# A trunk kernel on one core: the first shift and scale as TensorE products between projection steps, and a ring of 21 weight tiles

## The chip, the core and the metric

One Trainium2 chip, of which one core runs the whole program. The metric is the device time of one execution in microseconds (us). Three runs of the kernel before gave 1145.9, 1147.25 and 1149.82 us; the median is 1147.25.

## What is computed

One layer on 256 tokens of 1024 features, all float32. The conditioning vector c gives six rows (two shifts, two scales, two gates) of 1024 numbers each through one matrix of 1024 x 6144.

```python
mod = (jax.nn.silu(c) @ w_ada + b_ada).reshape(b, N_MOD, 1, d)
shift1, scale1, gate1, shift2, scale2, gate2 = (mod[:, i] for i in range(N_MOD))
h = rms_norm(x, norm1_g) * (1 + scale1) + shift1
proj = h @ w_in                                   # 1024 x 3078
# short convolution, stick-breaking attention and forgetting attention on parts of proj
x = x + gate1 * (y @ w_out)
h2 = rms_norm(x, norm2_g) * (1 + scale2) + shift2
return x + gate2 * moe_ffn(h2, ...)               # 32 experts, 4 for each token
```

## The kernel before

**Two stages.** The first (up to some 180 us) computes shift and scale, the normalized tokens, the projection, the three mixers, the output projection and the routing. The second goes through the 32 experts in order. The weights of one expert are twelve tiles of 1 MB (eight of the first matrix, four of the second), 128 partitions by 2048 numbers.

**The ring.** `big(kind, name)` gives a tile of 128 x 2048 out of one of four kinds, with the number of buffers in `KINDS` (line 33). The first stage uses the same buffers: kind "l" holds the tiles of `w_ada` (names a0 to a23) and `w_in` (w0 to w11), "h" the split projection weights and attention work tiles, "x" the normalized tokens and the like, "c" masks and the modulated tokens. The experts' tiles go round through the kinds in the order of the string `RING` (line 34), 20 long: tile n can be loaded when tile n - 20 has been used for the last time. `prefetch` issues the loads on SP's queue in program order, so a load that waits for a buffer holds up those behind it. An expert with more than 64 tokens has an extra block (`more`, for 32 tokens and further ones) that runs ahead of its ordinary pass and reads the same twelve tiles.

**The first projection.** Tokens are normalized (`xn`), turned on TensorE in four chunks of 256 features (`turn1(c)`, PSUM tile hTps), and modulated into `hT` with shift and scale of the chunk (`modulated1(c)`); `hT` is then split into two float32r parts, hTh by ScalarE and hTl by VectorE. `ada1(c)` gets the shift and the scale of one chunk on VectorE: `mod(m, c)` multiplies a half tile of `w_ada` with the row `silu_row` and adds up along it, four such passes in a chunk (line 236). A projection block (`Proj`, 256 columns of `w_in`) splits its weight tile into two parts (win0h, win0l, lines 109 and 110) and multiplies in 16 half steps of three products (`mm3`, 128 x 256 each, PSUM tile pr). `begin(c)` does the split, `steps(c, n)` the products up to chunk feature block n. `queue` fixes the order on TensorE: the products of a stage are issued after the last product of the stage ahead of it. The other engines' orders come from the scheduler of the framework. Loads are issued in the order of the string `order`.

Of the kernel before, what the change touches and what calls it, by code (L numbers as in the profile page):

```python
# [9 lines left out]
F32 = mybir.dt.float32  # L10
# [4 lines left out]
ALU = mybir.AluOpType  # L15
# [3 lines left out]
P = 128  # L19
# [10 lines left out]
CH = 2048  # L30


KINDS = {"l": 7, "h": 8, "x": 2, "c": 3}
RING = "lhhllccchlhhhxhhlllx"
CAP = 64
MORE = ((64, 32), (96, 64), (160, 64), (224, 32))

# [12 lines left out]
def trunk(ctx: ExitStack, tc: tile.TileContext, x_d, p1_d, p2_d, be_d, ada_d, win_d, wout_d, w1_d, w2_d, out_d):  # L50
# [8 lines left out]
    def big(kind, name):  # L59
        return ring.tile([P, CH], F32, tag=kind, bufs=KINDS[kind], name=name)  # L60

# [9 lines left out]
    def pa(name):  # L71
        return psA.tile([P, 2, 512], F32, tag="A", name=name)
# [9 lines left out]
    def mm(out, lhsT, rhs, start, stop):  # L82
        last[:] = [nc.tensor.matmul(out, lhsT, rhs, start=start, stop=stop, skip_group_check=True).ins]  # L83
# [101 lines left out]
    qkSB = big("x", "qkSB")  # L185
    v = big("x", "v").rearrange("p (t n) -> p t n", t=NT)
    ada, win, wout = {}, {}, {}
    order = "a0 a4 w0 a1 w6 a5 a2 a6 a3 a7 p0 w1 p1 w2 w3 w7 a8 a12 w4 a16 a9 w8 w5 a17 a10 a13 a11 w9 a14 a18 w10 a20 a15 w11 a19 a22 a23 a21 o1 o2 o3"
    for name in order.split():
        kind, c = name[0], int(name[1:])  # L190
        if kind == "p":
# [27 lines left out]
    nc.vector.tensor_mul(silu, silu, p1[:, C_C:C_C + KD])  # L219

    silu_row = t4o("silurow")
    ps = pa("silurow").rearrange("p b n -> p (b n)")
    for k in range(KD):
        mm(ps[:, k * P:(k + 1) * P], silu[:, k:k + 1].to_broadcast([P, P]), ident, True, True)
    nc.scalar.copy(silu_row[:, 0:512], ps[:, 0:512])
    nc.vector.tensor_copy(silu_row[:, 512:D], ps[:, 512:D])

    mods = const.tile([P, 6, KD], F32, name="mods")
    bada = p1[:, C_BC:C_BC + 48].rearrange("p (m k) -> p m k", m=6)
# [1 line left out]
    def mod(m, c):  # L231

        w = ada[4 * m + c].rearrange("p (i k) -> p i k", i=2)
        for i in range(2):
            k = 2 * c + i
            nc.vector.scalar_tensor_tensor(w[:, i], w[:, i], 1.0, silu_row, op0=ALU.mult, op1=ALU.mult,  # L236
                                           accum_out=mods[:, m, k:k + 1])
# [6 lines left out]
    def shift_scale(m, c, gain):  # L244

        biased(m, 2, c)
        cs = slice(2 * c, 2 * c + 2)
        nc.vector.scalar_tensor_tensor(mods[:, m + 1, cs], mods[:, m + 1, cs], 1.0, p1[:, gain + 2 * c:gain + 2 * c + 2],
                                       op0=ALU.add, op1=ALU.mult)
# [20 lines left out]
    def turn1(c):  # L270
        turned1[c] = pb(f"hTps{c}").rearrange("p (k s) -> p k s", k=2)
        for i in range(2):
            for t in range(NT):
                k = 2 * c + i
                turn(turned1[c][:, i, t * P:(t + 1) * P], xn[:, t, k * P:(k + 1) * P])

    def ada1(c):
        for m in range(2):
            mod(m, c)
        shift_scale(0, c, C_N1)  # L280

    def modulated1(c):

# [47 lines left out]
                                           gains[:, 2 * mixer + j:2 * mixer + j + 1],  # L331
                                           sq[:, j * S:(j + 1) * S], op0=ALU.mult, op1=ALU.mult)

    def two(t):
        return t[:, 0:768].rearrange("p (h s) -> p h s", h=2), t[:, 1024:1792].rearrange("p (h s) -> p h s", h=2)

    def sb_scores(pair):
        q, k = qk[0][:, 2 * pair, :], qk[0][:, 2 * pair + 1, :]
        ps = pa(f"sb{pair}")
        for blk in range(2):  # L340
            for j in range(2):
                r = slice(64 * j, 64 * j + 64)
                if blk == 0:
                    mm(ps[:, j, 0:256], k[r, 0:P], q[r, :], True, False)
                else:
                    mm(ps[:, j, 256:384], k[r, P:S], q[r, P:S], False, True)
        z = ps[:, :, 0:384]
        e, r = two(big("h", f"sbt{pair}"))
        nc.scalar.activation(e, z, AF.Abs)
        nc.scalar.activation(e, e, AF.Exp, scale=-1.0)  # L350
        nc.scalar.activation(e, e, AF.Ln, bias=1.0)
        nc.vector.scalar_tensor_tensor(r, z, 0.0, e, op0=ALU.max, op1=ALU.add)
        for b in (0, 2):
            blk_ = r[:, :, b * P:(b + 1) * P]
            nc.vector.tensor_mul(blk_, blk_, LT.rearrange("p (o s) -> p o s", o=1).to_broadcast([P, 2, P]))
        return ps, e, r
# [149 lines left out]
                   first and i == 0, last and i == len(ks) - 1)  # L506


    two_ps = pa("pr17")
    early = {}  # L510

    def begin(c, ps=None):
        early[c] = Proj(c, ps)

    def steps(c, n=KD):
        early[c].steps(n - early[c].k)

    queue(lambda: turn1(0),
          lambda: ada1(0),
          lambda: begin(0),  # L520
          lambda: turn1(1),
          lambda: modulated1(0),
          lambda: ada1(1),
          lambda: modulated1(1),
          lambda: begin(6),
          lambda: steps(0, 4),
          lambda: turn1(2),
          lambda: ada1(2),
          lambda: turn1(3),
          lambda: steps(6, 4),  # L530
          lambda: modulated1(2),
          lambda: ada1(3),
          lambda: steps(0, 6),
          lambda: modulated1(3),
          lambda: steps(6, 6),
          lambda: begin(1, two_ps[:, 0, :]),
          lambda: steps(1, 6),
          lambda: steps(0),
          lambda: steps(6),
# [562 lines left out]
def _layout(inp):  # L1102
# [34 lines left out]
    pick += [(256, 128), (512, 128), (384, 128), (640, 128), (0, 256)]  # L1137
    win = np.concatenate([w_in[:, a:a + n] for a, n in pick], axis=1)

    def blocks(w, n):  # L1140
        return w.reshape(KD, P, -1, n).transpose(2, 1, 0, 3).reshape(-1, P, KD * n)

    return {
        "x": f["x"][0], "p1": p1, "p2": np.stack([fw, rw]), "be": be,
        "ada": f["w_ada"][0].reshape(D, 24, 2, P).transpose(1, 3, 2, 0).reshape(24, P, CH), "win": blocks(win, 256),
        "wout": f["w_out"][0].reshape(4, 2, P, D).transpose(0, 2, 1, 3).reshape(4, P, CH),
        "w1": w1,
        "w2": f["w_mlp2"][0].reshape(NE, 4, 2, P, D).transpose(0, 1, 3, 2, 4).reshape(NE, 4, P, CH),
# [16 lines left out]
```

## Time and profile before

| | us |
|---|---|
| median of three runs | 1147.25 |
| the profiled execution | 1146.89 |
| span of its instructions | 1144.9 |
| PE busy (share of the span) | 1069.5 (93%) |
| DVE busy | 389.2 (34%) |
| ACT busy | 178.6 (16%) |
| mean transfer rate | 393 GB/s |

PE is TensorE's matmul side, DVE is VectorE, ACT is ScalarE, SP issues most loads. The profile is of one execution; a product's end is modelled, so two records that start 0.12 us apart can each be shown as 0.28 us long, and the spacing of starts is what a product costs. Float32 products are shown as two records each, float32r products as one. PEclk is the granted clock of TensorE: 1.00 is 2.4 GHz and 0.50 is 1.2 GHz.

### The profile page before, as it was taken

The numbers are of one execution on the slowest core, as the hardware profiler recorded it, in microseconds if no ns is written. First come the engines' busy times: TensorE is split into PE (matmuls) and PEld (weight loads), VectorE is DVE, ScalarE is ACT, GpSimd is POOL, SyncE is SP. The second block draws the span as 40 slices with busy tenths as digits, with TensorE's granted clock in tenths as the row PEclk, the third lists the DMA queues.
The fourth block names the chain that finished last, engine by engine and source line by source line (L and its number), as shares of the span: only waits on it lengthen the run. The fifth ranks groups of instructions, "written<-read, shape, count | busy, mean of one in ns | idle before, by whom it ended". The sixth has DMA issues, their size and how long they took to land. (4 is left out here: it accounts for less than half of the span.)

```text
span 1144.9 us, 14101 instructions
## 1 busy us (share of the span) xinstructions
PE 1069.5 (93%) x5432; PEld 467.1 (41%) x5432; DVE 389.2 (34%) x879; ACT 178.6 (16%) x412; POOL 14.5 (1%) x52
## 2 busy tenths in 40 slices
PE   2999999999989999999999989999999999898987
PEld 2887844343333333433333433434343434242322
DVE  7799933222232223222222222232232322231222
ACT  3458622010101010101010100101010101010100
POOL 1000000000000000000000000000000000000000
PEclk7899999999999999999999989999999999999999
DMA  9888899999987999999999999999999999999992
GB/s 383 360 297 311 331 409 370 416 418 417 418 353 309 417 418 417 418 418 417 417 418 416 419 399 404 419 418 418 417 417 419 417 418 417 411 416 410 416 413 110
DMA packets 62913, 449.54 MB, mean 393 GB/s; under 512 B 6960, under 2 KB 7472, under 8 KB 8624
## 3 DMA queue, kind: packets, MB, share of 16 engines
q1 hardware_dynamic: 62336, 447.11, 95.6%
q8 instruction: 79, 1.29, 0.5%
q10 hardware_dynamic: 432, 0.59, 0.1%
q14 instruction: 66, 0.54, 0.1%
HBM read 446.63 MB, written 1.05 MB: 391 GB/s over the span
## 5 line engine op out<-in xcount | busy, mean ns | idle before, releaser
L83 PE MATMUL u<-we,xg 128*64 128x512 f32 (+1 forms) x2304 | 494.2, 577 | 12.7 <-DMA we<-in_w 11.3
L83 PEld LDWEIGHTS u<-we,xg 128*64 128x64 f32 (+1 forms) x2304 | 154.0, 134 | 299.9 <-issue 260.4
L83 PE MATMUL o<-we,aT 128*64 128x512 f32 x1024 | 236.5, 598 | 3.7 <-DMA we<-in_w 3.3
L891 DVE TENSOR_SCALAR sw<-u 128x256 f32<-128x256 f32 (+1 forms) x68 | 28.3, 417 | 441.6 <-PE u L83 429.5
L892 ACT ACTIVATE sw<-sw 128x256 f32<-128x256 f32 (+1 forms) x68 | 27.9, 411 | 666.8 <-DVE sw L891 666.8
L83 PEld LDWEIGHTS o<-we,aT 128*64 128x64 f32 x1024 | 69.6, 136 | 133.2 <-issue 121.8
L1088 DVE TENSOR_TENSOR o<-o,g 64x512 f32<-64x512 f32 x64 | 44.1, 689 | 162.2 <-PE o L83 161.7
L83 PE MATMUL y<-o,sc 128*128 128x512 f32 (+1 forms) x160 | 67.1, 592 | 2.1 <-DVE o L1010 1.3
L83 PEld LDWEIGHTS xg<-oh,xn 128*128 128x128 f32 x512 | 58.6, 192 | 12.6 <-issue 12.4
L83 PE MATMUL xg<-oh,xn 128*128 128x128 f32 x512 | 62.1, 279 | 0.1
L236 DVE SCALAR_TENSOR_TENSOR a<-a,silurow 128x1024 f32<-128x1024 f32 x48 | 57.2, 1216 | 0.0
L745 DVE TENSOR_SCALAR xg<-xg,mods 128x128 f32<-128x128 f32 x64 | 26.0, 410 | 62.7 <-ACT xg L748 61.5
L83 PE MATMUL u<-b,pick 128*128 128x512 f32 x64 | 31.0, 484 | 17.3 <-PEq L1021 16.7
L83 PEld LDWEIGHTS y<-o,sc 128*128 128x128 f32 (+1 forms) x160 | 26.5, 197 | 41.8 <-issue 33.4
L944 DVE TENSOR_TENSOR xr<-xr,y 128x1024 f32<-128x1024 f32 x30 | 36.6, 1221 | 11.8 <-PE y L83 10.4
L904 ACT COPY aT<-aT 128x256 f32<-128x256 f32 x64 | 23.8, 372 | 106.1 <-PE aT L86 106.0
L748 ACT ACTIVATE xg<-xg,mods 128x128 f32<-128x128 f32 x64 | 28.9, 457 | 56.4 <-PE xg L83 45.9
L83 PEld LDWEIGHTS u<-b,pick 128*128 128x128 f32 x64 | 12.1, 189 | 57.1 <-issue 55.9
L86 PEld LDWEIGHTS aT<-ident,a 128*128 128x128 f32 x128 | 14.2, 141 | 50.7 <-issue 33.9
L895 DVE TENSOR_TENSOR a<-a,sw 128x256 f32<-128x256 f32 x64 | 27.4, 428 | 6.8 <-ACT sw L892 0.3
L86 PE MATMUL aT<-ident,a 128*128 128x128 f32 x128 | 27.2, 294 | 2.0
L83 PE MATMUL op<-o,yT 128*128 128x512 f32 x64 | 29.0, 600 | 0.0
(299 smaller groups left out, 750.3 us busy)
## 6 DMA issues: line engine op xcount, KB each, us to landing
we<-in_w SPq DMA_DIRECT2D x383, 1024.0 KB, 19.9
a<-in_ada SPq DMA_DIRECT2D x24, 1024.0 KB, 7.0
w<-in_win SPq DMA_DIRECT2D x12, 1024.0 KB, 11.0
o<-in_wout SPq DMA_DIRECT2D x4, 1024.0 KB, 5.8
xr<-in_x SPq DMA_DIRECT2D x1, 1024.0 KB, 5.3
we<-in_w SPq DMA_DIRECT2D x2, 512.0 KB, 18.1
b1in<-in_be SPq DMA_DIRECT2D x1, 512.0 KB, 5.3
out<-xr SPq DMA_DIRECT2D x2, 256.0 KB, 2.0
```

Source lines behind the costliest of these rows:

```text
L83: last[:] = [nc.tensor.matmul(out, lhsT, rhs, start=start, stop=stop, skip_group_check=True).ins]
L86: last[:] = [nc.tensor.transpose(out, in_, ident).ins]
L236: nc.vector.scalar_tensor_tensor(w[:, i], w[:, i], 1.0, silu_row, op0=ALU.mult, op1=ALU.mult, accum_out=mods[:, m, k:k + 1])
L745: nc.vector.tensor_scalar(o, x, s2[:, k:k + 1], t2[:, k:k + 1], op0=ALU.mult, op1=ALU.add)
L748: nc.scalar.activation(o, x, AF.Identity, scale=s2[:, k:k + 1], bias=t2[:, k:k + 1])
L891: nc.vector.tensor_scalar(gl, u[:, 0:n], 7.0, None, op0=ALU.min)
L892: nc.scalar.activation(sg, gl, AF.Sigmoid, scale=1.702)
L895: nc.vector.tensor_mul(ln, ln, sg)
L904: nc.scalar.copy(aT.rearrange("p j s -> p (j s)"), ps[:, 0:n])
L944: nc.vector.tensor_add(xr[:, t, :], xr[:, t, :], y.rearrange("p h m -> p (h m)"))
L1088: nc.vector.tensor_mul(o[64 * (e % 2):64 * (e % 2) + 64, 512 * h:512 * h + 512], ps[r, :], g2[r, :])
```

## The change

The first shift and scale leave VectorE. `ada1(c)` is now 32 products: for each of the eight blocks of the contraction and each of four groups q, the silu column repeated 32 times is the weight and a 128 x 128 piece of a `w_ada` tile (laid out anew on the host, so that a chunk's shift and scale lie in two tiles) is the data; the four groups write four bands of 32 partitions of one PSUM tile. A 32 x 32 block transpose on VectorE brings the sums to the features' partitions, and two small operations add the bias and the gain as before. `warm(n)` issues n products of the identity with itself into a PSUM bank that nobody reads. The products of `silu_row` move into the queue. The queue's stages and the order of the loads are new, and the ring has one "l" buffer more: 21 tiles in another order of kinds. `two` is renamed `halves`.

```diff
-KINDS = {"l": 7, "h": 8, "x": 2, "c": 3}
-RING = "lhhllccchlhhhxhhlllx"
+KINDS = {"l": 8, "h": 8, "x": 2, "c": 3}
+RING = "llhhllccchhhhxxhhllll"
...
-    order = "a0 a4 w0 a1 w6 a5 a2 a6 a3 a7 p0 w1 p1 w2 w3 w7 a8 a12 w4 a16 a9 w8 w5 a17 a10 a13 a11 w9 a14 a18 w10 a20 a15 w11 a19 a22 a23 a21 o1 o2 o3"
+    order = "a0 a1 w0 a2 a3 w6 a4 a5 w1 a6 a7 w7 p0 w2 p1 a8 a12 w3 a16 a9 w4 w8 w5 a17 a10 a13 a11 w9 a14 a18 w10 a20 a15 w11 a19 a22 a23 a21 o1 o2 o3"
...
+    two_ps = pa("pr17")
+    def warm(n):
+        for i in range(n):
+            mm(two_ps[:, 1, 0:P], ident, ident, True, True)
...
+    mods_ps = pa("mods")
     def ada1(c):
-        for m in range(2):
-            mod(m, c)
-        shift_scale(0, c, C_N1)
+        ps = mods_ps[:, c % 2, c // 2 * P:(c // 2 + 1) * P]
+        for k in range(KD):
+            w = ada[2 * c + k // 4].rearrange("p (k q n) -> p k q n", k=4, q=4)[:, k % 4]
+            for q in range(4):
+                mm(ps[32 * q:32 * q + 32, :], silu[:, k:k + 1].to_broadcast([P, 32]), w[:, q], k == 0, k == KD - 1)
+        t = sm.tile([P, P], F32, tag="sc", name=f"modsT{c}")
+        nc.vector.transpose(t, ps)
+        cs = slice(2 * c, 2 * c + 2)
+        nc.vector.tensor_tensor(mods[:, 0:2, cs], t.rearrange("p (m k i) -> p m k i", m=2, k=2)[:, :, :, 0],
+                                bada[:, 0:2, cs], op=ALU.add)
+        nc.vector.scalar_tensor_tensor(mods[:, 1, cs], mods[:, 1, cs], 1.0, p1[:, C_N1 + 2 * c:C_N1 + 2 * c + 2],
+                                       op0=ALU.add, op1=ALU.mult)
...
-    queue(lambda: turn1(0),
+    queue(lambda: warm(12),
+          silu_rows,
+          lambda: turn1(0),
+          lambda: turn1(1),
           lambda: ada1(0),
+          lambda: modulated1(0),
           lambda: begin(0),
-          lambda: turn1(1),
-          lambda: modulated1(0),
+          lambda: warm(8),
+          lambda: steps(0, 2),
+          lambda: warm(4),
           lambda: ada1(1),
           lambda: modulated1(1),
           lambda: begin(6),
+          lambda: warm(8),
+          lambda: turn1(2),
           lambda: steps(0, 4),
-          lambda: turn1(2),
+          lambda: steps(6, 2),
           lambda: ada1(2),
+          lambda: modulated1(2),
           lambda: turn1(3),
           lambda: steps(6, 4),
-          lambda: modulated1(2),
+          lambda: begin(1, two_ps[:, 0, :]),
+          lambda: steps(1, 4),
+          lambda: steps(0, 6),
           lambda: ada1(3),
-          lambda: steps(0, 6),
           lambda: modulated1(3),
           lambda: steps(6, 6),
-          lambda: begin(1, two_ps[:, 0, :]),
           lambda: steps(1, 6),
...
```

How the instructions move: TensorE at the start of the program, before (silurow is the silu row in PSUM, hTps a chunk of turned tokens, pr a projection block, xn the normalized tokens).

```order
L83 MATMUL silurow<-ident,silu 128x128 x8
L86 MATMUL hTps_265<-ident,xn 128x128 x4
L86 MATMUL hTps_283<-ident,xn 128x128 x4
L83 MATMUL pr_276<-hTh,win0h 128x256
L83 MATMUL pr_276<-hTl,win0h 128x256
```

The same place now (pr_234 is the PSUM tile that takes the fillers and the silu row, mods the sums of the new products, a_140 to a_148 tiles of `w_ada`).

```order
L83 MATMUL pr_234<-ident 128x128 x12
L83 MATMUL pr_234<-ident,silu 128x128 x8
L86 MATMUL hTps_277<-ident,xn 128x128 x4
L86 MATMUL hTps_282<-ident,xn 128x128 x4
L83 MATMUL mods<-a_140,silu 32x128 x16
L83 MATMUL mods<-a_142,silu 32x128 x16
L83 MATMUL pr_234<-ident 128x128 x8
L83 MATMUL pr_329<-hTh,win0h 128x256
```

Fillers and the first group of 32-column products now stand ahead of the first projection product; after twelve projection products four more fillers and the second group follow.

VectorE between the silu row and the second chunk, before (a_140 to a_152 are tiles of `w_ada`, w_144 and w_148 weight tiles that are split).

```order
L226 COPY silurow<-silurow 128x512
L236 SCALAR_TENSOR_TENSOR a_140,mods<-a_140,silurow 128x1024 x2
L236 SCALAR_TENSOR_TENSOR a_142,mods<-a_142,silurow 128x1024 x2
L110 TENSOR_TENSOR win0l<-w_144,win0h 128x1024
L242 TENSOR_TENSOR mods<-mods,p_74 128x2x2
L110 TENSOR_TENSOR win0l<-w_144,win0h 128x1024
L248 SCALAR_TENSOR_TENSOR mods<-mods,p_74 128x2
L236 SCALAR_TENSOR_TENSOR a_146,mods<-a_146,silurow 128x1024
L287 TENSOR_SCALAR hT<-hTps_265,mods 128x256 x2
```

And now.

```order
L237 COPY silurow<-pr_234 128x512
L110 TENSOR_TENSOR win0l<-w_144,win0h 128x1024 x2
L299 STREAM_TRANSPOSE modsT_319<-mods 128x128
L301 TENSOR_TENSOR mods<-modsT_319,p_74 128x2x2
L303 SCALAR_TENSOR_TENSOR mods<-mods,p_74 128x2
L311 TENSOR_SCALAR hT<-hTps_277,mods 128x256 x2
L313 TENSOR_TENSOR hTl<-hT,hTh 128x256 x2
L299 STREAM_TRANSPOSE modsT_392<-mods 128x128
L301 TENSOR_TENSOR mods<-modsT_392,p_74 128x2x2
L110 TENSOR_TENSOR win6l<-w_150,win6h 128x1024
L303 SCALAR_TENSOR_TENSOR mods<-mods,p_74 128x2
L110 TENSOR_TENSOR win6l<-w_150,win6h 128x1024
```

The passes over `w_ada` are gone from this stretch; the split of w0 now stands ahead of the first chunk's sums, and the split of w6 between the second chunk's sums and its hT.

## Rows read from the trace of the kernel before

**Rows 1.** The page's slices: the span in 40 equal parts of 28.6 us, GB/s moved.
```profile
GB/s 383 360 297 311 331 409 370 416 418 417 418 353 309 417 418 417 418 418 417 417 418 416 419 399 404 419 418 418 417 417 419 417 418 417 411 416 410 416 413 110
```
**Rows 2.** Stretches of the span: start and end, length, busy time (and instructions) of PE, PEld, DVE, ACT and POOL, granted clock, busy share of the sixteen transfer engines, GB/s.
```profile
35.00:58.70 23.70, 23.24 (x191) 21.40 (x190) 16.82 (x32) 10.70 (x18) 0.00 (x0) 1.00 0.81 326
58.70:171.00 112.30, 110.64 (x694) 83.50 (x693) 87.89 (x192) 66.07 (x143) 0.00 (x0) 1.00 0.90 342
180.00:340.00 160.00, 154.88 (x865) 61.54 (x865) 41.31 (x102) 17.57 (x44) 2.54 (x6) 1.00 1.00 409
342.00:349.00 7.00, 6.24 (x25) 2.10 (x26) 3.73 (x10) 0.00 (x0) 0.00 (x0) 0.76 0.01 4
356.00:640.00 284.00, 277.03 (x1269) 104.88 (x1269) 73.44 (x163) 26.68 (x67) 2.66 (x10) 1.00 1.01 418
1121.00:1134.00 13.00, 11.05 (x49) 3.25 (x47) 1.60 (x4) 0.79 (x2) 0.00 (x0) 1.00 0.07 30
```
**Rows 3.** Waits of SP's load queue between 310 and 352 us: for whom, us in total, times, longest.
```profile
SPq L858 <- PE u L83: 34.5, 6, 24.2
```
**Rows 4.** Timeline of PE between 303 and 352 us: start, length, engine, line, what it writes from what, count (xg gathers the tokens of the extra block; u with 64 columns is the ordinary pass).
```profile
323.00 1.07 PE L83 MATMUL xg<-xn,ox 128*32 128x256 f32 x16
...
344.68 0.47 PE L83 MATMUL u<-b,pick 128*128 128x512 f32 x1 [0.67 <-PEq L1021]
345.08 7.46 PE L83 MATMUL u<-we,xg 128*64 128x512 f32 x26
```
**Rows 5.** The chain that ended last, its end in order of time: start, length, what.
```profile
1112.57 19.88 DMA we<-in_w
1132.44 0.14 issue
...
1140.94 0.69 DVE xr L1098
```
**Rows 6.** The page's costliest groups: line, engine, operation, what from what, shape, count, busy us, mean ns of one, idle time before them.
```profile
L83 PE MATMUL xg<-oh,xn 128*128 128x128 f32 x512 | 62.1, 279 | 0.1
L236 DVE SCALAR_TENSOR_TENSOR a<-a,silurow 128x1024 f32<-128x1024 f32 x48 | 57.2, 1216 | 0.0
```
**Rows 7.** Timeline of PE in the first 36 us.
```profile
6.19 3.75 PE L83 MATMUL silurow<-ident,silu 128*128 128x128 f32 x16 [6.19 <-DVE silu L219]
...
10.37 1.04 PE L86 MATMUL hTps<-ident,xn 128*128 128x128 f32 x7 [0.21 <-DVE xn L265]
20.51 0.58 PE L83 MATMUL pr<-hTh,win0h 128*128 128x256 f32 x1 [9.10 <-ACT hTh L288]
22.00 0.58 PE L83 MATMUL pr<-hTl,win0h 128*128 128x256 f32 x1 [0.91 <-DVE hTl L289]
...
30.22 0.58 PE L83 MATMUL pr<-hTh,win0h 128*128 128x256 f32 x1 [5.51 <-ACT hTh L288]
```
**Rows 8.** Timeline of PE between 163 and 180 us (lg is the router's product, xg tokens gathered for the first two experts).
```profile
166.91 0.65 PE L83 MATMUL lg<-h2T,rw 128*32 128x128 f32 x16
...
174.36 1.06 PE L83 MATMUL xg<-oh,xn 128*128 128x128 f32 x8
```
**Rows 9.** The router's products by tile: ns of one (lowest, median, highest), first and last start.
```profile
L83 PE MATMUL lg<-h2T,rw x32: 272/273/298, 166.9 to 175.7; 128*32 128x128 f32 x32
```
**Rows 10.** Timeline of ACT between 13 and 31 us.
```profile
13.61 1.99 ACT L109 CAST win0h<-w 128x1024 fp32r<-128x1024 f32 x2 [3.04 <-DMA w<-in_win]
18.59 1.04 ACT L109 CAST win6h<-w 128x1024 fp32r<-128x1024 f32 x1 [2.99 <-DMA w<-in_win]
20.05 0.86 ACT L288 CAST hTh<-hT 128x256 fp32r<-128x256 f32 x2 [0.42 <-DVE hT L287]
```
**Rows 11.** Timeline of DVE between 13.5 and 31 us.
```profile
15.92 1.22 DVE L110 TENSOR_TENSOR win0l<-w,win0h 128x1024 fp32r<-128x1024 f32 x1
...
19.48 0.99 DVE L287 TENSOR_SCALAR hT<-hTps,mods 128x256 f32<-128x256 f32 x2
```
**Rows 12.** Groups of DVE between 300 and 350 us by shape: count, busy us, mean ns, idle before.
```profile
L953 DVE STREAM_TRANSPOSE xg<-xg 128x256 f32<-128x256 f32 x1 | 0.5, 451 | 0.0
```
**Rows 13.** Timeline of PE between 58 and 66 us (qkss is the sum of squares of two heads); pr<-hTh,win2h at 58.67 is the first product after the fourth projection block.
```profile
58.67 0.28 PE L83 MATMUL pr<-hTh,win2h 128*128 128x256 f32 x1
...
59.27 0.28 PE L83 MATMUL pr<-hTh,win2l 128*128 128x256 f32 x1
59.58 1.13 PE L83 MATMUL qkss<-qksq,masks 128*128 128x512 f32 x2
...
60.66 0.28 PE L83 MATMUL pr<-hTl,win2h 128*128 128x256 f32 x1
```
**Rows 14.** Stretches of 1 us, columns as in rows 2 (the granted clock is the third number from the end).
```profile
13.00:14.00 1.00, 0.00 (x0) 0.00 (x0) 1.00 (x3) 0.40 (x1) 0.00 (x0) 0.97 0.97 401
14.00:15.00 1.00, 0.00 (x0) 0.00 (x0) 1.00 (x3) 1.00 (x2) 0.00 (x0) 0.50 0.98 410
...
34.00:35.00 1.00, 1.00 (x9) 1.00 (x8) 1.00 (x4) 0.00 (x0) 0.00 (x0) 0.79 1.00 415
```
**Rows 15.** Waits of PE between 58 and 180 us: for whom, us in total, times, longest.
```profile
PE pr L83 <- DVE win5l L110: 0.8, 1, 0.8
...
PE pr L83 <- ACT win5h L109: 0.4, 1, 0.4
PE pr L83 <- DVE win3l L110: 0.3, 1, 0.3
```

More of the change, by code (lines that the diff above doesn't have):

```diff
@@ L221, in trunk, with silu_rows @@
     silu_row = t4o("silurow")
[L222 to L226, printed above, removed]
+    two_ps = pa("pr17")
+    def warm(n):
+        for i in range(n):
+            mm(two_ps[:, 1, 0:P], ident, ident, True, True)
+    def silu_rows():
+        ps = two_ps.rearrange("p b n -> p (b n)")
+        for k in range(KD):
+            mm(ps[:, k * P:(k + 1) * P], silu[:, k:k + 1].to_broadcast([P, P]), ident, True, True)
+        nc.scalar.copy(silu_row[:, 0:512], ps[:, 0:512])
+        nc.vector.tensor_copy(silu_row[:, 512:D], ps[:, 512:D])
     mods = const.tile([P, 6, KD], F32, name="mods")
@@ L275, in turn1 @@
                 turn(turned1[c][:, i, t * P:(t + 1) * P], xn[:, t, k * P:(k + 1) * P])
+    mods_ps = pa("mods")
     def ada1(c):
-        for m in range(2):
-            mod(m, c)
-        shift_scale(0, c, C_N1)
+        ps = mods_ps[:, c % 2, c // 2 * P:(c // 2 + 1) * P]
+        for k in range(KD):
+            w = ada[2 * c + k // 4].rearrange("p (k q n) -> p k q n", k=4, q=4)[:, k % 4]
[8 more added lines that the diff above has]
+                                       op0=ALU.add, op1=ALU.mult)
     def modulated1(c):
@@ L332, in qk_norm, with halves @@
                                            sq[:, j * S:(j + 1) * S], op0=ALU.mult, op1=ALU.mult)
-    def two(t):
+    def halves(t):
         return t[:, 0:768].rearrange("p (h s) -> p h s", h=2), t[:, 1024:1792].rearrange("p (h s) -> p h s", h=2)
@@ L347, in sb_scores @@
         z = ps[:, :, 0:384]
-        e, r = two(big("h", f"sbt{pair}"))
+        e, r = halves(big("h", f"sbt{pair}"))
         nc.scalar.activation(e, z, AF.Abs)
@@ L506, in out_proj @@
                    first and i == 0, last and i == len(ks) - 1)
-    two_ps = pa("pr17")
     early = {}
@@ L1138, in _layout @@
     win = np.concatenate([w_in[:, a:a + n] for a, n in pick], axis=1)
+    shift_scale = f["w_ada"][0][:, 0:2 * D].reshape(2, 4, P, 2, 4, 2, 4, 32)
+    shift_scale = shift_scale.transpose(4, 0, 2, 1, 6, 3, 5, 7).reshape(8, P, CH)
     def blocks(w, n):
@@ L1144, in _layout @@
         "x": f["x"][0], "p1": p1, "p2": np.stack([fw, rw]), "be": be,
-        "ada": f["w_ada"][0].reshape(D, 24, 2, P).transpose(1, 3, 2, 0).reshape(24, P, CH), "win": blocks(win, 256),
+        "ada": np.concatenate([shift_scale, f["w_ada"][0][:, 2 * D:].reshape(D, 16, 2, P).transpose(1, 3, 2, 0).reshape(16, P, CH)]),
+        "win": blocks(win, 256),
         "wout": f["w_out"][0].reshape(4, 2, P, D).transpose(0, 2, 1, 3).reshape(4, P, CH),
```

## Prediction

> **What bounds the kernel now.** I read the slices first. Loads run at 416 to 418 GB/s in most slices, but at 297 to 360 in four of the first five and at 353 and 309 in the two that meet at 343 us [rows 1]. So transfers are the limit for most of the span, and what has to be found is where they stop and what restarts them.
>
> The table of stretches answers that [rows 2]. From 180 to 340 us PE is busy 154.88 of 160 us, and its waits there name almost only its own branches, none a weight: PE sets the pace and the ring of weight tiles is full. From 342 to 349 us 4 GB/s are moved: the transfers stand still. SP sat 24.2 us on one product of the first expert layer [rows 3]: the extra block of 32 tokens (323.00 to 344.68 us) reads its expert's twelve tiles and the ordinary pass reads them again, so nothing is released until 345.08 plus four products at half clock [rows 4]. From 356 to 640 us the rate is 418 GB/s. At the end 30 GB/s, 0.07 of sixteen engines, run on from 1121 to 1134 us: one of the sixteen engines is about 13 us behind, though all had stopped together at 342 us. So from about 349 us to the last landing at 1132.44 us the slowest engine has work all the time, and some 10 us of products and additions follow [rows 5]. Two things move the end: **when PE releases the first tile after the stop**, and **how many tiles were loaded before it**. A stop that only some engines feel (near 680 us) moves nothing.
>
> Going back from there, PE has hardly a pause down to 35 us: busy 110.64 of 112.3 us and 23.24 of 23.7 [rows 2]. The chain therefore begins in the first 35 us, where VectorE is busy without a break: each shift or scale pass over half a tile takes 1216 ns, 16 such passes stand there [rows 6], and PE gets its first projection product at 20.51 us and the second chunk's at 30.22 us [rows 7].
>
> **The change, part by part.** The profiled execution took 1146.89 us (span 1144.9), 0.36 us under the median of 1147.25; the sum is made against 1146.89.
>
> *A. Shift and scale on PE.* Sixteen passes leave VectorE (16 x 1.216 = 19.5 us). Four groups of 32 products come, 32 columns of weights and 128 of data. The router's products have exactly this shape: 16 records (8 products) in 0.65 us, each lasting 0.273, so (0.65 - 0.273)/15 = 0.025 us a record, 0.05 us a product at full clock, and a group 1.6 us [rows 8, 9]. A filler is a 128 x 128 product: 0.22 us at full clock (8 records in 1.06 us, each 0.279), 0.47 at half clock (8 in 3.75) [rows 6 to 8].
>
> The first chunk: w0 is still the fourth MB in the queue, so its casts still start at 13.61; w0 and w6 are two loads and 4.98 us apart, 2.5 us a load [rows 10]. The first subtraction can start at 14.65, the second ends at 17.0 (1.2 us each [rows 11]); VectorE's transpose of 128x256 takes 451 ns [rows 12], so I take 0.25 for 128x128, plus 0.15 for two small operations, 0.5 for hT and 0.43 for its cast: the first projection product starts at 18.3 instead of 20.51. The fillers and the first group are over by about 14.8 (turned tiles 11.4, group 1.6, eight fillers 1.8), so PE then stands 3.5 us.
>
> The second chunk waits for 12 products, 4 fillers and its group. At full clock that is 18.3 + 0.45 (wait for hTl) + 1.45 + 0.9 + 1.6 = 22.7; with the first two at half clock 24.8; with all at half clock 26.4. VectorE then needs transpose and small operations 0.5, both halves of w6 (they stand ahead of hT in its order) 2.3, hT 0.5, and the cast 0.43: 3.7 us. PE starts on the second chunk at 26.4, 28.5 or 30.1.
>
> From there PE is dense. 180 products x 0.12 = 21.6 (spacing of [rows 13]); two more groups 3.2; a turn 0.5; waits for hTl 0.7; the forget gate's eight products, of twice the router's columns, 0.8, its turn with the wait for ScalarE's copy 1.3 (an estimate from the copies' 0.4 us); two qkss 1.9 (less than twice 1.15); changes of product kind some 0.6: 30.6 us. The end is 57.0, 59.1 or 60.7. Before, the same work ends at 58.67 plus 1.15 for the second qkss (59.27 to 60.66 less two spacings) [rows 13]: 59.8. So A gives +2.8, +0.7 or -0.9 us. It is small because PE, relieved of waiting, takes on 6.4 us of groups itself, and most of the 30 us are needed either way. I take **+0.7**: the granted clock fell to 0.50 at 13.9 us, 2.6 us after PE's last product, and came back only at 34.4 us, after PE had worked from 30.2 us [rows 14]; a gap of 3.5 us is nearest to that. Ends: -1.5 and +2.8.
>
> The Trainium skill, "TensorE: Matmul & The Clock Gate", Part 3, gives 3.07x for four tiles packed by rows and 2.38x for three packed by columns, not the full number. By that a group would cost 32 x 0.22/3.07 = 2.3 us, an estimate from that page, and A would be lower by about 2 us; the rows of this trace show 0.22/0.05 = 4.4x for this very shape, so the sum goes by them.
>
> *B. What follows.* Between 58 and 171 us PE waits 0.8, 0.4 and 0.3 us for splits of w5 and w3 [rows 15]. VectorE has its split of w7 done near 46 us (after hT of the last chunk near 43) instead of 53.4, does w2 and four gate passes (2.4 + 4.9) while PE is in the fourth block, and waits some 3 us for the forget gate; it so reaches w3 about 2 us earlier. I count **+1.0** of the 1.5; ends 0 and 1.5. The order inside that stage changes little, and its loads get earlier.
>
> *C. One more tile.* At 342 us the queue stands for 7 us, and one more load takes 2.5 us, so it fits into the stop; every later release then serves a tile one place further on. From there the slowest engine is never idle, so the end comes **2.5 us** earlier; ends 0 and 2.5. What hides the tile before 300 us is that PE waits for no weight there: the earlier loads themselves win nothing. For the same reason the new order of kinds costs nothing: SP now comes to both x buffers as 14th and 15th tile and waits there until the output projection is through with its weights (near 167 us), with the l tiles behind it, where it waited at the 16th before; without that cover each load held back would cost 2.5 us.
>
> Moved loads: a2 and a3 stand ahead of w6, w1 and w7 ahead of the gates. Each is wanted later than its place times 2.5 us says (a7 lands at 33.6, PE wants it near 40). Layout work on the host and the renamed helper cost nothing on the device.
>
> Sum: 0.7 + 1.0 + 2.5 = 4.2, so 1142.7, and on the scale of the median **1143.0 us**; own range 1141 to 1145.
>
> **The rivals.**
> 1. *The fillers do not hold the clock.* PE's pause after 14.8 us lets it fall, and 12 products, 4 fillers and the whole group run at 1.2 GHz: A is -0.9 and B shrinks to 0.6; 2.2 us remain, 1145.0. For it: [rows 14]; the products that began at 22.0 us did not raise it before [rows 7]. Against: work would start earlier and be longer. The same page of the Trainium skill, Part 1, has half rate as the default that activity releases and idleness brings back. By that rule, with which the rows agree, the first filler groups are spent for nothing. Chance 0.20.
> 2. *The tile counts nothing.* If transfers, not releases, bind from 180 us on, or the slowest engine is idle again later, C is 0 and 1.7 us remain: 1145.5. Against: 4 GB/s over 7 us. Chance 0.10.
> 3. *All goes well.* The clock stays full, the waits for splits vanish: 2.8 + 1.5 + 2.5 = 6.8, 1140.5. Chance 0.14.
> 4. *Slower: the 32-column products do not overlap.* At 0.22 us a product a group costs 7.0 instead of 1.6 us on PE, with the projection steps queued behind it; the first has some 4 us of room, so 1.4 + 3 x 5.4 = 17.6 us later: 1160.6. It turns the sign past the 3.4 us of "no change" from about 0.13 us a product. Against: the router's 0.05. Chance 0.08.
>
> **How the numbers follow.** The forecast has 0.48. A measurement here can tell about 0.3% (3.4 us) from no change, so "faster" is below 1143.8: about two thirds of the forecast (0.33), rival 3 (0.14) and a little of the first two (0.02): 0.49. Same: the rest of the forecast and of rivals 1 and 2: 0.43. Slower: rival 4, 0.08. The range reaches from the third rival less 1.7 us (runs spread by some 2 us to either side) to the case in which A is -1.5 and C is 0, with such a spread: 1138.8 to 1147.5.
>
> **What would show it.** A: no passes of 1.2 us on VectorE for the first two rows; groups of 64 records in 1.6 us; second chunk near 28.5 us; the last product of the fourth projection at about 54.5 us (the forget gate now behind it), and second qkss done near 59. B: no waits for w3 and w5. C: the stop at 342 us some 2.5 us shorter, and 418 GB/s after it. Wrong: a group over 3 us, a stop that does not shorten, or PE waiting for weights before 340 us.

## The result: 0.6% slower, where 0.4% faster was forecast

The changed kernel takes 1154.38 us (median of six executions, 1151.93 to 1156.67); the kernel before takes 1147.35 in six (1145.9 to 1149.82). The ratio is 1.0058, 95% interval 1.004 to 1.0076: slower by some 6.7 us. The forecast was 1143.0, range 1138.8 to 1147.5; a slower kernel had been given 0.08, for another reason.

The execution profiled of the changed kernel took 1151.93 us (its shortest), 5.04 more than the one profiled before. Page and stretches of the changed kernel, columns as in [rows 1, 2]:

```profile
span 1150.2 us, 14703 instructions
PE 1086.3 (94%) x5752; PEld 481.2 (42%) x5752; DVE 372.5 (32%) x851; ACT 178.7 (16%) x412; POOL 14.5 (1%) x52
GB/s 381 416 236 329 337 381 340 419 418 400 417 417 236 408 419 417 418 419 417 416 418 417 419 415 408 418 418 419 417 417 418 413 415 408 415 413 412 415 411 107
```

```profile
35.00:58.70 23.70, 23.22 (x240) 21.38 (x239) 15.96 (x29) 7.15 (x12) 0.00 (x0) 1.00 1.02 417
56.20:61.71 5.51, 3.54 (x23) 1.53 (x22) 2.19 (x7) 3.88 (x10) 0.00 (x0) 1.00 1.00 415
183.00:340.00 157.00, 151.07 (x772) 59.96 (x775) 40.41 (x100) 16.94 (x41) 2.54 (x6) 0.99 0.98 403
346.00:357.00 11.00, 9.59 (x47) 3.50 (x41) 5.62 (x14) 0.00 (x0) 0.00 (x0) 0.69 0.04 12
363.00:640.00 277.00, 272.20 (x1244) 101.89 (x1243) 73.17 (x162) 26.27 (x66) 2.66 (x10) 1.00 1.01 417
```

The stop is still there (12 GB/s) and again 417 GB/s follow, but it comes later. VectorE has 16.7 us less work than before, TensorE 16.8 us more. Timeline of PE at the start, to be held against [rows 7]:

```profile
1.55 4.67 PE L83 MATMUL pr<-ident 128*128 128x128 f32 x24 [1.55 <-POOL ident masks.py:199]
11.36 1.96 PE L83 MATMUL mods<-a,silu 128*32 128x128 f32 x64
13.24 2.05 PE L83 MATMUL pr<-ident 128*128 128x128 f32 x16
18.82 0.57 PE L83 MATMUL pr<-hTh,win0h 128*128 128x256 f32 x1 [3.52 <-ACT hTh L312]
...
23.01 1.95 PE L83 MATMUL mods<-a,silu 128*32 128x128 f32 x64
...
28.84 0.39 PE L83 MATMUL pr<-hTh,win0h 128*128 128x256 f32 x1 [1.46 <-ACT hTh L312]
```

Up to the second chunk it went nearly as forecast: first product 18.82 (18.3 said), second chunk 28.84 (28.5), before 30.22. A group lasts 1.88 us from its first record to the next kind of product (11.36 to 13.24), against 1.6 said; that is 1.88/32 = 0.059 us a product, 3.7 to one against a filler's 0.22. The router's rows [rows 8, 9] had given 4.4 to one. The 3.07x for four tiles packed by rows in the Trainium skill, "TensorE: Matmul & The Clock Gate", Part 3, from which 2.3 us had been estimated, is lower than the 3.7 measured here.

From 56 us on things went otherwise. PE, and beside it DVE and ACT (flog and flogt belong to the forget gate); [rows 13] show the same place before:

```profile
56.24 1.06 PE L83 MATMUL flog<-hT,fw 128*32 128x256 f32 x14
57.79 0.61 PE L83 MATMUL flogt<-SELE,flogp 128*128 128x6 f32 x4 [0.48 <-ACT flogp L421]
58.26 1.96 PE L83 MATMUL qkss<-qksq,masks 128*128 128x512 f32 x4
61.71 0.39 PE L83 MATMUL pr<-hTh,win2h 128*128 128x256 f32 x1 [1.49 <-DVE qkSB L354]
```

```profile
59.38 0.17 DVE L434 SCALAR_TENSOR_TENSOR logf<-f,g 128x12 f32<-128x12 f32 x1 [0.77 <-ACT g L433]
60.78 0.88 DVE L354 SCALAR_TENSOR_TENSOR qkSB<-pr,gains,qksq 128x256 f32<-128x256 f32 x2 [1.24 <-ACT qksq L179]
```

```profile
47.77 0.60 ACT L348 ACTIVATE qksq<-pr 128x512 f32<-128x512 f32 x1 [2.29 <-PE pr L83]
59.40 0.69 ACT L178 ACTIVATE qksq<-qkss,epsc 128x512 f32<-128x512 f32 x1
```

The squares of the first projection block are ready at 48.37, but TensorE's order now has their sum (qkss) behind the fourth block and the forget gate. So VectorE takes the block out of its PSUM tile (qkSB) only at 60.78, and the block of w2, which needs that tile, waits 1.49 us. Before, that sum stood at the start of the fourth block, and VectorE had the tile free at 55.57, 3.1 us ahead of w2:

```profile
52.18 1.02 PE L83 MATMUL qkss<-qksq,masks 128*128 128x512 f32 x2
54.69 0.88 DVE L330 SCALAR_TENSOR_TENSOR qkSB<-pr,gains,qksq 128x256 f32<-128x256 f32 x2
```

w2 now starts at 61.71 instead of 58.67. Of TensorE's waits between 56 and 182 us, to be held against [rows 15], the two longest beside that one (pv is a product of the mixers):

```profile
PE pv L83 <- ACT xn L178: 1.6, 1, 1.6
PE pr L83 <- ACT win5h L109: 1.0, 1, 1.0
```

Then the start of the expert stage, PE, and the code queue among the transfers from 187 to 190 us (packets, MB, share of 16 engines). "issue" is time in which TensorE waited for nothing that the profile shows, and PEq is its sequencer:

```profile
182.71 0.47 PE L86 MATMUL og<-ident,og 128*128 128x128 f32 x1
187.07 0.47 PE L83 MATMUL u<-b,pick 128*128 128x512 f32 x1 [0.39 <-PEq L1052]
187.48 1.93 PE L83 MATMUL u<-we,xg 128*64 128x512 f32 x7
190.70 5.79 PE L83 MATMUL u<-we,xg 128*64 128x512 f32 x25 [1.29 <-issue]
196.43 0.51 PE L83 MATMUL u<-b,pick 128*128 128x512 f32 x1
...
216.80 0.64 PE L83 MATMUL o<-we,aT 128*64 128x512 f32 x1 [0.59 <-issue]
```

```profile
q8 instruction: 1, 0.02, 2.1%
```

The first half of the first expert's first matrix (four tiles) took from 187.07 to 196.43, 9.36 us, where before it took 7.42; in the middle TensorE stands for 1.29 us and waits for nothing that the profile shows. A packet of program code falls into these 3 us; others do so in kernels without a pause, as e9 will show. The granted clock just before (third number from the end):

```profile
183.00:184.00 1.00, 1.00 (x5) 0.90 (x5) 0.96 (x7) 0.00 (x0) 0.00 (x0) 0.50 1.03 434
185.00:186.00 1.00, 1.00 (x6) 1.00 (x6) 0.00 (x0) 0.78 (x3) 0.00 (x0) 0.50 1.02 426
```

Last, the pass after the stop and the chain's end [rows 4, 5]:

```profile
352.20 0.77 PE L83 MATMUL u<-b,pick 128*128 128x512 f32 x1 [0.66 <-PEq L1052]
```

```profile
1117.90 19.89 DMA we<-in_w
1137.79 0.14 issue
...
1146.28 0.69 DVE xr L1129
```

The pass starts 7.52 us later (344.68 before), the last landing comes only 5.35 later.

**Where the 7.52 us arise**, by the differences of these starts: 3.15 up to the turn of the slots (og, 182.71 against 179.56), 1.13 from there to the first expert (half clock), 1.94 within the first half of the first expert, 0.81 in the rest of it (0.59 is a pause at its end, 216.80), 0.49 until and at the stop (clock 0.69 there). From the pass to the end of the execution it is 1151.93 - 352.20 = 799.73 instead of 1146.89 - 344.68 = 802.21.

### The profile page after: what moved, and what is told of

Its sections match the earlier page's. It is cut to its first block, busy times and chain, and to the rows that moved or that the text cites. A ratio compares the mean times of both kernels' runs of the same rounds, so it can differ in the third digit from the quotient of the medians.

```text
span 1150.2 us, 14703 instructions
## 1 busy us (share of the span) xinstructions
PE 1086.3 (94%) x5752; PEld 481.2 (42%) x5752; DVE 372.5 (32%) x851; ACT 178.7 (16%) x412; POOL 14.5 (1%) x52
## 3 DMA queue, kind: packets, MB, share of 16 engines
HBM read 446.63 MB, written 1.05 MB: 389 GB/s over the span
## 5 line engine op out<-in xcount | busy, mean ns | idle before, releaser
L247 DVE SCALAR_TENSOR_TENSOR a<-a,silurow 128x1024 f32<-128x1024 f32 x32 | 38.1, 1217 | 0.0
```

## The experiments

The table has, for the profiled execution of each kernel, the start of the first projection product, of the turn of the slots (og), of the product with the biases (`u<-b,pick`) that opens the first and the second half of the first expert, and of the pass after the stop, all in us (the expectations call these two halves, of four tiles each, the first expert's eight tiles and the next expert); the execution; the difference of the last two; and the ratio of all its executions to those of the kernel before on the same chip.

| kernel | product | og | half 1 | half 2 | pass | execution | rest | ratio (95%) |
|---|---|---|---|---|---|---|---|---|
| before | 20.51 | 179.56 | 182.79 | 190.21 | 344.68 | 1146.89 | 802.2 | |
| changed | 18.82 | 182.71 | 187.07 | 196.43 | 352.20 | 1151.93 | 799.7 | 1.0058 (1.004 to 1.0076) |
| e1_ring_alone | 20.50 | 179.68 | 182.91 | 190.33 | 344.79 | 1144.27 | 799.5 | 0.9968 (0.9957 to 0.998) |
| e2_old_ring | 18.68 | 184.29 | 188.62 | 198.51 | 354.05 | 1156.18 | 802.1 | 1.0078 (1.0056 to 1.01) |
| e3_norm_early | 18.59 | 181.02 | 185.29 | 195.28 | 350.81 | 1150.50 | 799.7 | 1.0029 (1.0016 to 1.0042) |
| e4_no_fillers | 15.84 | 183.46 | 187.72 | 195.20 | 350.23 | 1150.00 | 799.8 | 0.9995 (0.9984 to 1.0005) |
| e5_split_behind | 15.94 | 182.92 | 186.16 | 198.52 | 354.05 | 1154.04 | 800.0 | 1.0026 (1.0016 to 1.0037) |
| e6_first12_only | 18.67 | 184.32 | 188.58 | 195.99 | 353.79 | 1153.10 | 799.3 | 1.0042 (1.003 to 1.0054) |
| e7_later20_only | 15.88 | 182.35 | 186.60 | 194.01 | 349.09 | 1148.34 | 799.3 | 1.0007 (0.9996 to 1.0018) |
| e8_no_fill_early | 16.09 | 183.02 | 187.25 | 194.66 | 349.18 | 1148.24 | 799.1 | 0.9992 (0.9983 to 1.0) |
| e9_24_fillers | 18.65 | 184.19 | 187.43 | 194.85 | 349.37 | 1148.71 | 799.3 | 1.0033 (1.002 to 1.0046) |
| e10_route_fillers | 15.82 | 180.21 | 183.45 | 190.87 | 345.91 | 1145.75 | 799.8 | 1.0 (0.9989 to 1.001) |
| e11_ring_19 | 20.46 | 180.01 | 183.25 | 190.67 | 345.11 | 1150.32 | 805.2 | 1.0025 (1.0015 to 1.0036) |
| e12_no_fill_norm | 15.88 | 177.13 | 181.38 | 188.80 | 343.42 | 1143.30 | 799.9 | 0.9985 (0.9973 to 0.9997) |
| e13_norm_route | 15.80 | 179.17 | 182.35 | 189.77 | 344.83 | 1144.24 | 799.4 | 0.9968 (0.9958 to 0.9979) |
| e14_norm_route_w5 | 15.84 | 177.59 | 180.77 | 188.19 | 346.38 | 1145.98 | 799.6 | 0.9994 (0.9984 to 1.0003) |

**The ring.** e1 puts the new `KINDS` and `RING` alone into the kernel before, e2 puts the old ones into the changed kernel, e11 is the kernel before with 19 tiles:

```diff
-KINDS = {"l": 7, "h": 8, "x": 2, "c": 3}
-RING = "lhhllccchlhhhxhhlllx"
+KINDS = {"l": 6, "h": 8, "x": 2, "c": 3}
+RING = "llhhlccchhhhxxhhlll"
```

> The kernel before with nothing changed but the ring: 21 tiles and the new order of kinds. Theory (one more 2.5 us load fits into the stop at 342 us, and the slowest transfer engine has work from there to the end): 2.5 us under the kernel before, ratio 0.9978, last landing about 1130 instead of 1132.4, and no landmark of TensorE before 320 us moved. Rival 1 (the tile counts nothing): ratio 1.000. Rival 2 (both x tiles as 14th and 15th hold the loads behind them, and the start of the expert stage waits for weights): TensorE's landmarks move between 180 and 200 us, 3 to 5 us slower, ratio 1.003 to 1.004.

> The changed kernel with the ring of 20 and the old order of kinds. Theory: 2.5 us over the changed kernel, 1156.9, ratio to the kernel before 1.0083; TensorE's landmarks up to 320 us stay at those of the changed kernel (second projection block at 61.7, first expert at 187). Rival (the new ring is what made the start of the expert stage late): first expert near 185, total 1149 to 1151, ratio 1.002 to 1.003.

> The kernel before with a ring of 19 tiles (one l buffer less), in an order of kinds like the new one. In the ten kernels run so far the time from the ordinary pass after the stop to the end of the execution was 802.2 us with 20 tiles (two kernels) and 799.1 to 800.0 with 21 (eight kernels). Theory (each tile in the ring is one load of 2.5 us that the slowest transfer engine need not do after the stop): 804.7 us, total 2.5 us over the kernel before, ratio 1.0022. Rival (what mattered is the order of kinds): as before or faster, ratio 1.000 or less.

The column "rest" is the answer: 805.2 with 19 tiles, 802.1 and 802.2 with 20, 799.1 to 800.0 in thirteen kernels with 21. A tile more is 2.5 to 3 us less behind the stop, and the landmarks of e1 ahead of it moved by 0.1 us. So the tile is worth what was forecast. e1's median is 1144.25. In e2 the landmarks did move (first expert 188.62, 187 said), and the intervals of its ratio and the changed kernel's overlap; there only the rest speaks.

The way to it was another than forecast. The stop, and what the load queue had moved up to 349.5 us (packets, MB, share), before and then in e1:

```profile
341.50:349.50 8.00, 7.04 (x28) 2.50 (x29) 4.20 (x11) 0.00 (x0) 0.00 (x0) 0.79 0.01 3
q1 hardware_dynamic: 18128, 127.80, 91.2%
```

```profile
341.50:349.50 8.00, 7.04 (x27) 2.41 (x27) 4.32 (x11) 0.00 (x0) 0.00 (x0) 0.79 0.01 3
q1 hardware_dynamic: 18272, 128.85, 92.2%
```

The stop is as long as before, 8 us. The 1.05 MB more, one tile, were moved ahead of it, 0.96 of them by 180 us.

**The norm of the first block.** e3 puts it back into the fourth block, a quarter into it:

```diff
...
+          lambda: steps(7, 2),
+          lambda: qk_norm(early[0].ps, 0),
           lambda: steps(7))
...
-    qk_norm(early[0].ps, 0)
```

> The changed kernel with the norm of the first projection block (its sum of squares and its product on VectorE) put into the queue after a quarter of the fourth block, as it stood before the change; the forget gate stays behind the fourth block. Theory (TensorE waits 1.5 us at the block of w2 for the PSUM tile that this norm must read first): that wait is gone, the block starts near 59.7 instead of 61.7, and the 2 us stay to the end: 1152.4, ratio 1.0044. Rival (the next waits, at w5 and at the start of the expert stage, take it back): 1154.4, ratio 1.006.

PE in e3:

```profile
59.26 0.39 PE L83 MATMUL pr<-hTh,win2h 128*128 128x256 f32 x1
```

The wait at w2 is gone, w2 starts 2.45 us and og 1.69 us earlier, and the ratio falls by 0.29% (some 3.3 us; more than the 2 expected, and the intervals overlap from 1.004 to 1.0042).

**The fillers.** e4 leaves out all 32, e6 the later 20, e7 the first 12 (`warm` with no products, or left out of the queue); e5 keeps all and ties the split of w0 behind the first chunk's hT on VectorE, and that of w6 behind the second's:

```diff
-          lambda: begin(0),
+          lambda: begin_behind(0, 0),
...
-          lambda: begin(6),
+          lambda: begin_behind(6, 1),
...
+            made[c] = nc.vector.tensor_scalar(hT[:, k, :], tr, s1[:, k:k + 1], t1[:, k:k + 1], op0=ALU.mult, op1=ALU.add).ins
...
+    def begin_behind(c, chunk):
+        with tc.issue_after(made[chunk]):
+            begin(c)
```

> The changed kernel without the 32 filling products. Theory (the fillers neither hold the clock for the first twelve products nor stand much in the way): the second chunk starts within 1 us of 28.8, but TensorE runs it at half clock for some us; total within 1.5 us of the changed kernel, ratio 1.0045 to 1.007. Rival 1 (the fillers are in the way): second chunk near 26, total near 1151, ratio 1.003. Rival 2 (they do hold the clock in the second chunk): 1157 or more, ratio over 1.008. Apart from these, code for TensorE is then fetched at other places, and the 1.3 us in which TensorE waited for nothing visible in the first expert should be gone or elsewhere.

> The changed kernel with all its fillers, but VectorE's two split passes over w0 are put behind the first chunk's hT, and those over w6 behind the second chunk's (an edge of order, no other instruction moved by hand). Without fillers the scheduler had made that order itself, and the first projection product started at 15.84 instead of 18.82 us. Theory (the fillers cost mainly through the order that the scheduler then gives VectorE): first product near 16.2, second chunk at 25 to 26.5 instead of 28.8, total 1150 to 1152, ratio 1.003 to 1.0045. Rival (the fillers' own 10 us on TensorE are the cost): second chunk at 28 or later, total 1154, ratio 1.006.

> The changed kernel with the twelve fillers at the start of the program alone; the 8, 4 and 8 between the projection steps are left out. VectorE's order keeps the split of w0 ahead of the first chunk's sums, so the first product stays at 18.8. Theory (order): the cost of the first twelve is 3 us at the first product, and the second chunk comes at 25 to 26; total 1149 to 1151. Rival (the fillers between the steps are all of the cost): total 1145.9 as without fillers.

> The changed kernel without the first twelve fillers; the 8, 4 and 8 between the projection steps stay. The split of w0 is then behind the first chunk's hT on VectorE. Theory (order): first product at 16, second chunk near 25, total 1148 to 1150. Rival 1 (these twenty are harmless): as without fillers, 1145.9 or less. Rival 2 (these twenty are the cost): 1153 to 1154.

Leaving the fillers out was worth 0.63%, 7.2 us, far more than I expected. Most of it is the first twelve: they alone (e6, 1.0042) cost 0.47% over e4, the later twenty alone (e7, 1.0007) 0.12%, within the noise. e6's median, 1153.1, is over the 1149 to 1151 of its theory, with the second chunk at 26.49 (25 to 26 said); e7's, 1148.62, is as its theory said. DVE in the changed kernel, and then without fillers:

```profile
14.76 2.36 DVE L110 TENSOR_TENSOR win0l<-w,win0h 128x1024 fp32r<-128x1024 f32 x2 [3.77 <-ACT win0h L109]
17.04 0.31 DVE L299 STREAM_TRANSPOSE modsT<-mods 128x128 f32<-128x128 f32 x1
```

```profile
13.22 0.32 DVE L299 STREAM_TRANSPOSE modsT<-mods 128x128 f32<-128x128 f32 x1 [2.06 <-PE mods L83]
13.96 0.99 DVE L311 TENSOR_SCALAR hT<-hTps,mods 128x256 f32<-128x256 f32 x2
14.88 1.22 DVE L110 TENSOR_TENSOR win0l<-w,win0h 128x1024 fp32r<-128x1024 f32 x1
```

With the first twelve fillers the scheduler has VectorE wait 3.77 us for the cast of w0 while the finished sums (13.24 us) stand behind it; without them it takes the sums first, and the first product starts at 15.8 to 16.1 instead of 18.6 to 18.8. That holds in all five kernels with the first twelve and the scheduler's order, and in all seven without them; e5 has the twelve, and the other order by its edge alone, and wins 0.32% (3.7 us) with every filler in place. The theory of order was right, but it is about half of the whole. In e5's trace the second chunk starts at 24.68 and the block of w2 at 59.29, 2.42 us earlier than in the changed kernel, though PE now waits for w1 (0.73 us) and w2's wait stays. Yet og comes at 182.92, no earlier. Between the two the clock fell, where in the changed kernel it is full:

```profile
92.00:98.00 6.00, 5.24 (x25) 4.53 (x26) 6.00 (x11) 5.75 (x14) 0.00 (x0) 0.50 0.84 309
```

It also has the longest pause in the first expert, 12.36 us for the half.

Two things limit what the traces of e4 and e5 say: each is of the longest execution of its kernel (1150.00 and 1154.04), the changed kernel's of its shortest, so that none shows the 7.2 us as a whole; and the mean clock differs, 0.987 over the changed kernel's six executions and 0.991 over e4's twelve. Among e4's own, 0.992 to 0.993 goes with 1144.98 to 1146.28 us, and 0.987 to 0.988 with 1149.68 to 1150.00. How much of the fillers' price is the clock, no run here parts from the order and the pause.

**The pause in the first expert.** From half 1 to half 2 it is 7.41 to 7.48 us in twelve kernels and 9.36, 9.89, 9.99 and 12.36 in the four with 32 fillers ahead (changed, e2, e3, e5). e9 leaves out the eight behind the second group, where TensorE waits anyway:

> The changed kernel without the last eight fillers (those after the second group), which stand where TensorE waits for the second chunk anyway; the order on VectorE is the changed kernel's. So far the first expert's eight weight tiles took 7.4 us of TensorE in every kernel with 0, 12 or 20 fillers and 9.4 to 12.4 us in the four with 32, with a pause that no semaphore explains and a packet of program code on its way. Theory (32 fillers put a boundary between two pieces of code just behind the branch into the first expert; with 24 it lies elsewhere): 7.4 us again, no pause, the next expert 20.15 instead of 20.7 to 21.2 us; total 2 to 3 us under the changed kernel, ratio 1.003 to 1.004. Rival (the pause comes from the late start of the stage, or from the clock): 9.4 us or more, ratio 1.0055.

PE in e9, and its code queue from 187 to 191 us:

```profile
184.19 0.33 PE L86 MATMUL og<-ident,og 128*128 128x128 f32 x1
187.43 0.47 PE L83 MATMUL u<-b,pick 128*128 128x512 f32 x1 [0.69 <-ACT xg L778]
187.83 7.09 PE L83 MATMUL u<-we,xg 128*64 128x512 f32 x32
194.85 0.50 PE L83 MATMUL u<-b,pick 128*128 128x512 f32 x1
```

```profile
q8 instruction: 1, 0.02, 1.6%
```

7.42 us again, 20.14 for the rest, no pause, although this execution came to og 1.48 us later than the changed kernel: not the late start made the pause. The ratio falls to 1.0033 (the intervals overlap). A code packet comes here too, as in the kernel before between 185 and 186 us, so the packet in the changed kernel proves nothing by itself.

Over the whole traces the place of such pauses (over 1 us, ended by no engine and no transfer) goes with the number of products that were added, and kernels with the same number agree. With 32 they end at 189 to 193 us and come nowhere else; with 24 at 436, 463 and 628, with 20 at 462, with 15 (e14) at 268, with 12 at 276, with 7 (e10, e13) there is none, and with none added (e4, e8, e12) the first ends at 485 to 492. The kernel before has them as well:

```profile
485.82 0.47 PE L83 MATMUL u<-b,pick 128*128 128x512 f32 x1 [1.99 <-PEq L1021]
```

Behind the stop they cost nothing that can be seen: the rest is 799.1 to 800.0 with them and without. Shown is that the pause's place goes with the instructions ahead; that it is code which arrives late fits this, but is not shown.

**Gate and norm without fillers; the pauses in the routing.** e8 is e4 with the norm as in e3 and the forget gate ahead of the last steps of the second block; e10 is e4 with products of the identity in the routing's pauses:

```diff
+          lambda: fill(3),
           lambda: route(1),
...
+          lambda: fill(4),
           lambda: place(1),
```

> No fillers, and the forget gate and the norm of the first projection block are in the queue where they stood before the change (the gate ahead of the last steps of the second block, the norm after a quarter of the fourth). Theory (the two savings are of different waits and add up): 3.4 us (the norm put early in the changed kernel) and about 0.5 us (wait for ScalarE's copy in the forget gate) under the kernel without fillers: 1142 to 1143, ratio 0.996 to 0.9965, and the block of w2 starts near 58. Rival (what TensorE gains before 60 us it loses at w3, w5 and at the start of the expert stage): 1145.5, ratio 0.999.

> The kernel without fillers at the start, but with three and four products of the identity in the two pauses of TensorE in the routing (0.5 us for ScalarE's copy, 0.7 us for VectorE's choice of experts). All eight kernels with the new first stage showed the clock at half for some 3.4 us between 181 and 191 us, the two with the old stage did not. Theory (it is these pauses that let the clock fall): no half clock between 180 and 192 us, and 1.1 us less from the second token half's places to the first expert (3.2 instead of 4.3 us); total 1 to 1.7 us under the kernel without fillers, ratio 0.998 to 0.9985. Rival (the fall comes from elsewhere, or the products only delay the routing): the half clock stays, ratio 0.9995 to 1.0005.

Both theories fell. e8 gained nothing that can be measured: its trace has half clock near 19, 26, 36 and 94 us. In e10's trace the half clock at the stage's start is gone (3.24 us from og to the first expert, as theory said), but the executions are no shorter, and e9's trace has none there either without such products.

**What is left.** e12 is e3 without fillers, e13 adds e10's products, e14 eight more ahead of the block of w5:

```diff
-    a5 = proj(5)
+    p5 = Proj(5)
+    queue(lambda: fill(8), p5.steps)
+    a5 = p5.ps
```

> No fillers, and only the norm of the first projection block put back into the fourth block (the forget gate stays behind it). Theory (the wait of 1.5 us at w2 is the same wait with and without fillers, and worth about as much as in the changed kernel): 2 to 3 us under the kernel without fillers, ratio 0.997 to 0.998, and the block of w2 starts near 59. Rival (TensorE was made to run ahead into a clock at half: without fillers the time won before 60 us comes back as stretches at half clock before 110 us): ratio 0.9985 to 0.9995 as for the version with gate and norm moved, with two or more such stretches in the trace between 17 and 110 us.

> The kernel with no fillers at the start and with the norm put back into the fourth block, and with three and four products of the identity in TensorE's two pauses in the routing. Theory (the slow executions have a half clock that these pauses let in): no half clock between 175 and 192 us, and the executions, which went from 1142.1 to 1149.2 without these products, keep within 4 us; median 1144 to 1145, ratio 0.9965 to 0.9975. Rival (the half clock comes anywhere, with the phase of the execution): the spread stays at 6 us or more and the median at 1146, ratio 0.998 to 0.999.

> The same, and eight products more in TensorE's pause ahead of the block of w5 (1.0 and 0.8 us in the traces). Theory: no half clock between 85 and 110 us either, which four of the thirteen traces showed; median 1143 to 1144.5, ratio 0.9955 to 0.997. Rival 1 (these products stand in the way): the block of w5 starts 1 us later and the total is 1 us over the run beside this one. Rival 2 (phase): spread of 6 us or more, ratio 0.998 to 0.999.

e12's executions go from 1142.13 to 1149.19, its four shortest with a mean clock of 0.991 to 0.993, its seven longest with 0.987 to 0.990; the median gained 0.1% on e4, less than theory said. e13 reaches 0.9968 (1144.34), level with e1, and these two beat both kernels most clearly (e12's interval ends at 0.9997); it spans 1141.79 to 1146.46: narrower, if not within 4 us; its interval overlaps e12's. e14 filled the pause at w5 and lost 2.3 us, but not at w5: its og comes at 177.59, 1.58 earlier than e13's. PE in e14, some experts on:

```profile
263.58 2.74 PE L83 MATMUL o<-we,aT 128*64 128x512 f32 x12
268.14 0.49 PE L83 MATMUL u<-b,pick 128*128 128x512 f32 x1 [1.82 <-PEq L1063]
268.56 8.78 PE L83 MATMUL u<-we,xg 128*64 128x512 f32 x32
```

A pause of 1.82 us at a branch, and then half clock (0.50 from 270 to 272 us; 8.78 instead of 7.09). e6 has the same at 276 us (2.02 us). So eight products more went with such a pause in a kernel that had none.

**Open:** what sets the clock's fall in one execution and not in the next of the same kernel; what the pauses are; and the 2.4 us between the changed kernel's profiled execution and its median.

## Why the prediction was wrong

- *What bounds the kernel:* right. The execution is the start of the pass after the stop plus a time that, within 1 us in all sixteen, depends on the number of tiles alone.
- *C, one more tile, +2.5:* the size right, 2.5 in the traces (802.21 to 799.73); the way to it wrong. The tile was to fit into the stop and shorten it by 2.5 us, and a stop that does not shorten was named as a sign of being wrong. In e1 it does not shorten: the tile is loaded ahead of it. In the changed kernel the stop is even longer, 10 us.
- *A, +0.7:* the first two landmarks nearly right, size too large by 1.1. The last product of the fourth block starts at 56.03 instead of about 54.5, and the second qkss is over at about 60.2 (58.26 and 1.96) instead of 59.1. Groups of 1.88 for 1.6 are 0.6 of it in the two that count; before, the end was 59.8, so A is -0.4, inside its ends. The price of 32-column products (rival 4) held. Rival 1 held in part: the clock was 0.50 from 19 to 22 us, but not over the second group.
- *B, +1.0, ends 0 and 1.5:* **this step failed**, sign and range. It listed the splits that TensorE had waited for and asked whether VectorE would be early. It put the forget gate and both qkss behind the fourth block as TensorE time, and did not ask who waits for what comes out of them: the PSUM tile of w2's block hangs on that norm (1.49 us). Nor did the waits for w5 go: 1.0 us against 1.2 before, and 0.3 for w3 as before; and a `pv` now waits 1.6 us for ScalarE's root of a head's norm. From 59.8 to og the change lost 2.75 us: 3.15 less A's 0.4. TensorE's waits there add up to 5.6 us against 3.4, which is 2.2 of it; e3 shows the part of the norm.
- *Not in the sum:* "the order inside that stage changes little", and nothing at all between 180 and 345 us. **That was the largest miss:** 3.88 us were lost at the start of the experts (1.13 at half clock, 1.94 and 0.81 with the pauses) and 0.49 at the stop. The prediction asked there only whether weights would come late.

Together -0.4 - 2.75 - 3.88 - 0.49 + 2.48 = -5.04, the difference of the two executions. The changed kernel's median is 2.4 us over its profiled execution, that of the kernel before 0.5 over its own. The fillers were priced at what they take of TensorE, 1.8 and 0.9 us. Their price, 7.2 us by e4, is in part VectorE's order (e5), which I had read in the listing and taken as given, and in part the pause that came with them (e9); the share of the clock is open.

## What to carry to other kernels

Where an order is made by a scheduler, read what it does to the release of each buffer, not just to the busy time: a small product put late can hold the tile that the next block needs. Price a filler by what it moves, the order of the other engines and the pauses behind it, and try the kernel with the fillers alone taken out. Measure the parts of a change apart: here one line (the ring) was worth 0.3% and the rest of the change took back nearly three times that.

## What the runs showed that I had not expected

- Pauses of 1.0 to 2.9 us on TensorE that no engine and no transfer ends, in fourteen kernels of sixteen, at places that go with the number of products ahead. Ahead of the stop, where TensorE sets the pace, they fall in six; the kernel before has its own behind it, at 486, 513, 652 and 708 us.
- After such a pause the clock can fall: 8.78 us for 32 records that take 7.09 (e14).
- A weight tile more in the ring took 2.5 us off the end, with a stop in the transfers that stayed as long.
- The old first stage has the clock at half from 14 to 34 us [rows 14] and then at full up to the stop, in all three of its traces, so that its half clock falls where TensorE mostly waits. The new one has it at full earlier and falls back in stretches of which the place changes from trace to trace, in the first stage and at the start of the experts.
